# A decoder layer's residual stream kept in DRAM through its mixer, with the attention's output added there by transfers

## The chip, the cores and the metric

The kernel runs on one core of a Trainium2 chip. The metric is the device time of one execution in microseconds (us); lower is better. A core has a matrix engine (TensorE, PE in the profile; its weight loads are PEld), a vector engine (VectorE, DVE), an activation engine (ScalarE, ACT), a general engine (GpSimd, POOL) and a queue engine (SyncE, SP). Transfers are issued from SP, ACT or POOL and run on 16 DMA engines.

## The reference

One decoder layer on x of 512 tokens by 1024 channels, in float32. Each `rms_norm` is a root-mean-square norm.

```python
x = x + 0.5 * swiglu(rms_norm(x, norm_ffn1_w), ffn1_w_in, ffn1_w_out)
x = x + hybrid_mixer(rms_norm(x, norm_mix_w), ...)
x = x + memory_cross_attention(rms_norm(x, norm_cross_w), rms_norm(mem, norm_mem_w), ...)
x = x + 0.5 * swiglu(rms_norm(x, norm_ffn2_w), ffn2_w_in, ffn2_w_out)
return rms_norm(x, norm_final_w)
```

The mixer has two parts that share an input and an output projection: a state-space scan with 16 heads in 4 groups (with a depthwise convolution and a gate z), and differential attention with 8 heads:

```python
z, xbc, dt_raw, q, k, v = split_sizes(h @ w_in, IN_SIZES)
...
return jnp.concatenate([y_ssd, y_attn], axis=-1) @ w_out
```

## The kernel before

**Tiles.** The residual stream x lies transposed: eight tiles of 128 channels by 512 tokens, `x[0]` to `x[7]`, two by two in four pair tiles `x2` of 128x1024. The stream is "column o" for `x[o]`. Each product is done in three float32r matmuls, since each operand is split into a high and a low part (`wh`, `wl` for weights: `wh` by ScalarE at L154, `wl` by VectorE at L155). A weight tile arrives by a load on SP's queue into one of six buffers `wr` (L173).

**Order.** `Order` interleaves two kinds of generators: `od.add` queues dense work (projections), `od.spawn` starts side chains that take a step when the dense work has come far enough by an estimate of matmul time. SP and POOL execute in exactly the order in which the code names their instructions. For PE, DVE and ACT a scheduler picks the order from its own estimates. Each engine then runs its list strictly in order and waits at semaphores.

**Buffers.** Products go into PSUM banks: `acc` has four, `aux` four. Most working tiles are 128x512 and come from the pool `sp` by `s2`, 53 slots (`NSLOT`) under one tag, handed on when the last reader is done. A pool's tag has buffers of its own that no other tag uses.

**The work around the change**, in the order of the dense queue: the first FFN ends with column updates and `fin1`, which spawns `normed` (the mixer's norm, making the eight tiles `h`) and `block_sums_in_dram`, a background chain: SP copies blocks of the second FFN's weights into DRAM tiles `isum` and `wsum` (L1224) and POOL adds other blocks to them there by accumulating transfers (L1228). Then come the cross memory's keys, `queries_keys`, `values`, the groups of the scan (`group_dense`, `group`) and, between them, `out_attn(hg, o0, o1)`: the attention half `hg` (four heads) times its rows of the output projection, columns o0 to o1-1, each a product `pm` of 12 matmuls (weights `woa`), which VectorE adds to `x[o]` (L840). It is called for (0, 0 to 8) after group 0, (1, 0 to 5) after group 1, and (1, 5 to 8) after group 3. Next `memory_values` makes the cross memory's values (products `pcv`, weights `wcv`), and `out_proj` with `upd_c` projects the scan's outputs `ys` (weights `wos`), adds them to `x[o]` (L1092) and makes the cross attention's input from it. Between the norm of the mixer and `upd_c` nothing reads x but these adds.

In a scan group, the chain on POOL is `ysq` (the sum of two squares, L992) and `ncol` (a power, L379), on which later matmuls wait; `pst`, `pf`, `py` are small matmuls, `st` the scan's state, and `conv` (L857) begins the convolution of a product `pxbc`. In the attention heads POOL computes `rr`.

Of the kernel before, what the change touches and what calls it, by code (L numbers as in the profile page):

```python
# [11 lines left out]
F32 = mybir.dt.float32  # L12
R32 = mybir.dt.float32r
AF = mybir.ActivationFunctionType
ALU = mybir.AluOpType
AX = mybir.AxisListType

P = 128
T = 512
D = 1024  # L20
KT = D // P
# [78 lines left out]
def body(tc, a, dbg=None):  # L100
    nc = tc.nc
    ctx = ExitStack()
    ctx.enter_context(tc.manual_schedule(engines={mybir.EngineType.SP, mybir.EngineType.Pool}))
    cp = ctx.enter_context(tc.tile_pool(name="cp", bufs=1))
    wp = ctx.enter_context(tc.tile_pool(name="wp", bufs=3))
    sp = ctx.enter_context(tc.tile_pool(name="sp", bufs=NSLOT))
# [3 lines left out]
    dram = ctx.enter_context(tc.tile_pool(name="dram", bufs=1, space=bass.MemoryType.DRAM))  # L110
# [3 lines left out]
    def nm(s):  # L114
        uid[0] += 1
        return f"{s}_{uid[0]}"

    def s2(s, dt=F32, shape=(P, T)):
        if math.prod(shape[1:]) <= T // 2:
            return sp.tile(list(shape), dt, tag="s1", name=nm(s), bufs=NHALF)  # L120
        return sp.tile(list(shape), dt, tag="s2", name=nm(s))
# [7 lines left out]
    def acc(s, shape=(P, T)):  # L129
        return acc_p.tile(list(shape), F32, tag="acc", name=nm(s))  # L130
# [4 lines left out]
    def dump(name, t):  # L135
        if dbg and name in dbg:
            nc.sync.dma_start(dbg[name], t.bitcast(F32) if t.dtype == R32 else t)

    last, start, last_sum, recent, newest, newest_lo, newest_mm = [], [], [], [], [], [], []
    V, S, G = nc.vector, nc.scalar, nc.gpsimd  # L140
    od = Order()
# [9 lines left out]
    def split_into(hi, lo, src, scale=None):  # L151
        if scale is None:
            return (
                S.activation(hi, src, AF.Copy),  # L154
                V.tensor_tensor(lo, src, hi.bitcast(F32), ALU.subtract),  # L155
            )
        return (
            S.activation(hi, src, AF.Copy, scale=scale),
            V.scalar_tensor_tensor(lo, src, scale, hi.bitcast(F32), ALU.mult, ALU.subtract),
        )  # L160

    def split(s, src, scale=None, half=False, n=T):
        if half:
            both = s2(s, R32, (P, 2, T // 2))
            hi, lo = both[:, 0], both[:, 1]
        else:
            hi, lo = s2(s + "h", R32, (P, n)), s2(s + "l", R32, (P, n))
        last[:] = [i.ins for i in split_into(hi, lo, src, scale)]
        return hi, lo

    def load_w(src, n=D):
        raw = wp.tile([P, n], F32, tag="wr", name=nm("wr"), bufs=6)
        nc.sync.dma_start(raw, src)  # L173
        hi = wp.tile([P, n], R32, tag="wh", name=nm("wh"))
        lo = wp.tile([P, n], R32, tag="wl", name=nm("wl"))
        with ExitStack() as after:
            for i in start:
                after.enter_context(tc.issue_after(i))
            recent[:] = [i.ins for i in split_into(hi, lo, raw)]
        return hi, lo  # L180
# [152 lines left out]
    def mm3(ps, w, x, first, last, wc=slice(None), xc=slice(None)):  # L333
        (wh, wl), (xh, xl) = w, x
        mm(ps, wh[:, wc], xh[:, xc], first, False)
        mm(ps, wh[:, wc], xl[:, xc], False, False)
        mm(ps, wl[:, wc], xh[:, xc], False, last)

    def proj(ps, w, xs, ks=None):
        n = len(xs)  # L340
        for k in ks or range(n):
            mm3(ps, w, xs[k], k == 0, k == n - 1, wc=slice(k * P, (k + 1) * P))
            yield
# [2 lines left out]
    par = cp.tile([P, NPAR], F32, name="par")  # L346
    nc.sync.dma_start(par, a["par"])
    x, wa = [], []
    x2 = [cp.tile([P, 2, T], F32, name=f"x{k}") for k in range(KT // 2)]
    for k in range(KT):  # L350
        xk = x2[k // 2][:, k % 2]
        (S if k == 0 else nc.sync).dma_start(xk, a["xT"][k])
# [62 lines left out]
    def make_h(k, c):  # L415
        return split("hm", x[k], par[:, c + k : c + k + 1])

    def normed(st, c, dst):

        yield from st.finish()  # L420
        hf = {}
        for k in range(KT + 1):
            if k < KT:
                hf[k] = s2("hf")
                V.scalar_tensor_tensor(hf[k], x[k], par[:, c + k : c + k + 1], st.row, ALU.mult, ALU.mult)
            if k > 0:
                dst.append(split("hn", hf.pop(k - 1)))
                yield 1.6
# [140 lines left out]
    with tc.issue_after(start[0]):  # L569
        for k in range(KT):  # L570
            st1.add(x[k])
    st_mix, h = Stat(), []

    def beside(ti):
        if ti == 0:
            od.spawn(memory_norm())
        elif ti == 2:
            od.spawn(memory_prep(hm, 2.5), 10.0)

    def fin1(o):  # L580
        st_mix.add(x[o])
        if o == KT - 3:
            od.spawn(normed(st_mix, C_MIX, h), 3.0)
            od.spawn(block_sums_in_dram(), 60.0)

    od.spawn(st1.finish(), 18.0)
    od.add(ffn1(h1, wa_s, fin1, beside))


# [244 lines left out]
    def out_attn(hg, o0, o1):  # L834
        yield lambda: all(y is not None for y in ya[4 * hg : 4 * hg + 4])
        heads = ya[4 * hg : 4 * hg + 4]
        for o in range(o0, o1):
            po = acc("pm")
            yield from proj(po, load_w(a["woa"][hg, o], 4 * P), heads)
            V.tensor_tensor(x[o], x[o], po, ALU.add)  # L840
        if o1 == KT:
            ya[4 * hg : 4 * hg + 4] = [None] * 4

# [208 lines left out]
    def memory_values():  # L1052
        pv = [[acc("pcv") for _ in range(2)] for _ in range(2)]
        def part(k, w, tb, n):
            mm3(pv[tb][n], hm2[k], w, k == 0, k == KT - 1, wc=slice(tb * P, (tb + 1) * P), xc=slice(n * T, (n + 1) * T))

        banks = [(tb, n) for tb in range(2) for n in range(2)]
        for k in range(KT - 2):
            w = load_w(a["wcv"][k])
            for tb, n in banks:  # L1060
                part(k, w, tb, n)
                yield
        ws = [load_w(a["wcv"][k]) for k in range(KT - 2, KT)]
        for tb, n in banks:
            for j in range(2):
                part(KT - 2 + j, ws[j], tb, n)
                yield
            if n == 0:
                cv.append([])
            cv[tb].append(split("cv", pv[tb][n], st_mem.col[:, tb : tb + 1]))  # L1070
        hm2.clear()
# [17 lines left out]
    st_c, h_c = Stat(), []  # L1089

    def upd_c(o, po):
        V.tensor_tensor(x[o], x[o], po, ALU.add)  # L1092
        h_c.append(make_h(o, C_CROSS))
        st_c.add(x[o])
        dump(f"x2_{o}", x[o])
        if o == KT - 1:
            h.clear()
            od.spawn(st_c.finish(), 3.0)
# [6 lines left out]
    for hd in range(1, 4):  # L1105
        od.add(queries_keys(hd))
    od.add(group_dense(0))
    od.add(out_attn(0, 0, 8))
    od.add(queries_keys(4))
    od.add(values(1))  # L1110
    for hd in range(5, 8):
        od.add(queries_keys(hd))
    od.add(group_dense(1))
    od.add(out_attn(1, 0, SPLIT))
    od.add(group_dense(2))
    od.add(group_dense(3))
    od.add(out_attn(1, SPLIT, 8))
    od.add(memory_values())
    od.add(out_proj(ys, a["wos"], lambda: all(y is not None for y in ys), upd_c))


# [89 lines left out]
    def block_sums_in_dram():  # L1211
        jobs = []
        for c, (f0, nf) in enumerate(THIRDS):
            gs = range(f0 // 2, (f0 + nf) // 2)
            jobs += [(isum[g][0], a["f2q"][g][0], a["f2q"][g][1]) for g in gs]
            jobs += [(isum[g][1], a["f2q"][g][2], isum[g][0]) for g in gs]
            blocks, sums = a[f"f2b{c}"], wsum[c]
            for t, (to, more) in enumerate(((blocks[B12], blocks[B11]), (blocks[B12], blocks[B22]), (blocks[B22], sums[0]), (blocks[B21], sums[2]))):
                for k in range(0, nf // 2 * T, D):
                    ks = slice(k, min(k + D, nf // 2 * T))  # L1220
                    jobs.append((sums[t][:, ks], to[:, ks], more[:, ks]))
        for n in range(len(jobs) + LEAD):
            if n < len(jobs):
                nc.sync.dma_start(jobs[n][0], jobs[n][1])  # L1224
                yield 4.5
            if n >= LEAD:
                to, _, more = jobs[n - LEAD]
                G.dma_start(to, more, accum_op=ALU.add, max_dma_last_dim=4 * D)  # L1228
                yield 8.0
# [262 lines left out]
```

## Time and profile before

| | |
|---|---|
| Three runs | 1307.47, 1308.36, 1309.42 us |
| Profiled execution | 1306.71 us, span 1304.7 us |
| Instructions in the span | 20807 |
| Mean granted TensorE clock | 0.998 |
| Moved by DMA | 229.03 MB, mean 176 GB/s |
| HBM | read 225.53 MB, written 50.91 MB |

The span goes from the first to the last instruction. In the lines of the profile, "busy" is time in which an engine has work, and a name such as `x<-x,pm` says what an instruction writes and reads, buffer numbers left out. Waits are given as total, times and longest. A "q" behind an engine's name marks an instruction of its sequencer, such as the issue of a transfer.

### The profile page before, as it was taken

The numbers are of one execution on the slowest core, as the hardware profiler recorded it, in microseconds if no ns is written. First come the engines' busy times: TensorE is split into PE (matmuls) and PEld (weight loads), VectorE is DVE, ScalarE is ACT, GpSimd is POOL, SyncE is SP. The second block draws the span as 40 slices with busy tenths as digits, with TensorE's granted clock in tenths as the row PEclk, the third lists the DMA queues.
The fourth block names the chain that finished last, engine by engine and source line by source line (L and its number), as shares of the span: only waits on it lengthen the run. The fifth ranks groups of instructions, "written<-read, shape, count | busy, mean of one in ns | idle before, by whom it ended". The sixth has DMA issues, their size and how long they took to land.

```text
span 1304.7 us, 20807 instructions
## 1 busy us (share of the span) xinstructions
PE 1292.8 (99%) x8108; PEld 1150.9 (88%) x8108; DVE 969.6 (74%) x1520; ACT 695.3 (53%) x1183; POOL 108.9 (8%) x127
## 2 busy tenths in 40 slices
PE   9999999999999999999999999999999999999997
PEld 7889999999987788887888888888899999989995
DVE  6886888788884787548877796656677878877886
ACT  6444654556553666336564564434465645555564
POOL 1010010000010011200101012020011000000001
PEclk9999999999999999999999999999999999999999
DMA  8156667767664434953468379594239875655662
GB/s 310 49 192 170 191 166 196 186 182 195 186 232 151 129 90 118 265 182 93 117 182 246 105 174 260 188 225 143 69 106 253 223 229 168 191 201 172 191 204 91
DMA packets 69729, 229.03 MB, mean 176 GB/s; under 512 B 8616, under 2 KB 12176, under 8 KB 69280
## 3 DMA queue, kind: packets, MB, share of 16 engines
q1 hardware_dynamic: 52832, 176.26, 38.7%
q0 software_dynamic: 13056, 44.65, 18.9%
q10 hardware_dynamic: 3744, 6.82, 1.7%
q8 instruction: 63, 1.03, 0.3%
q14 instruction: 34, 0.28, 0.1%
HBM read 225.53 MB, written 50.91 MB: 212 GB/s over the span
## 4 chain that ended last, share of the span: by engine, by line
PE 90%; issue 6%; DVE 2%; ACT 1%; POOL 1%; POOLq 0%; ACTq 0%; DVEq 0%
PE qb L252 15%; PE pm L145 10%; PE qa L252 10%; PE qe L252 10%; PE pxbc L145 5%; PE pcq L145 3%; PE pz L145 3%; PE po L145 3%; PE ob L1258 3%; PE pv L145 3%; PE oa L1258 2%; PE pq L145 2%; PE oe L1258 2%; PE pk L145 2%; PE pa L145 2%
## 5 line engine op out<-in xcount | busy, mean ns | idle before, releaser
L154 ACT ACTIVATE wh<-wr 128x1024 fp32r<-128x1024 f32 (+2 forms) x323 | 329.3, 1022 | 355.6 <-issue 95.7
L155 DVE TENSOR_TENSOR wl<-wr,wh 128x1024 fp32r<-128x1024 f32 (+2 forms) x323 | 379.7, 1178 | 144.6 <-ACT wh L154 138.6
L145 PE MATMUL pxbc<-hnh,wh 128*128 128x512 f32 x128 | 52.9, 413 | 0.0
L252 PE MATMUL qb<-s24h,wl 128*128 128x256 f32 x184 | 52.2, 284 | 0.2 <-DVE wl L155 0.2
L252 PE MATMUL qb<-s24h,wh 128*128 128x256 f32 x184 | 52.4, 285 | 0.0
L252 PE MATMUL qb<-s24l,wh 128*128 128x256 f32 x184 | 52.2, 284 | 0.0
L252 PE MATMUL qb<-s31h,wh 128*128 128x256 f32 x184 | 52.2, 283 | 0.0
L252 PE MATMUL qe<-s31h,wh 128*128 128x256 f32 x184 | 52.1, 283 | 0.0
L252 PE MATMUL qb<-s31l,wh 128*128 128x256 f32 x184 | 52.1, 283 | 0.0
L252 PE MATMUL qe<-s24l,wh 128*128 128x256 f32 x184 | 52.1, 283 | 0.0
L252 PE MATMUL qe<-s24h,wh 128*128 128x256 f32 x184 | 52.1, 283 | 0.0
L252 PE MATMUL qb<-s31h,wl 128*128 128x256 f32 x184 | 52.1, 283 | 0.0
L252 PE MATMUL qe<-s31l,wh 128*128 128x256 f32 x184 | 52.1, 283 | 0.0
L252 PE MATMUL qe<-s24h,wl 128*128 128x256 f32 x184 | 52.1, 283 | 0.0
L252 PE MATMUL qe<-s31h,wl 128*128 128x256 f32 x184 | 52.1, 283 | 0.0
L145 PE MATMUL pxbc<-hnh,wl 128*128 128x512 f32 x128 | 50.2, 392 | 0.0
L145 PE MATMUL pxbc<-hnl,wh 128*128 128x512 f32 x128 | 49.9, 390 | 0.0
L754 ACT ACTIVATE ec<-ec,mn 128x512 f32<-128x512 f32 (+3 forms) x64 | 35.5, 556 | 25.7 <-DVE mn L753 25.6
L252 PE MATMUL qa<-h11h,wh 128*128 128x256 f32 x152 | 43.1, 283 | 0.0
L252 PE MATMUL qa<-h11h,wl 128*128 128x256 f32 x152 | 43.0, 283 | 0.0
L252 PE MATMUL qa<-h11l,wh 128*128 128x256 f32 x152 | 43.0, 283 | 0.0
L860 DVE SCALAR_TENSOR_TENSOR conv<-pxbc,par,conv 128x511 f32<-128x511 f32 (+2 forms) x48 | 35.8, 746 | 6.5 <-ACT conv L857 5.7
(490 smaller groups left out, 4171.0 us busy)
## 6 DMA issues: line engine op xcount, KB each, us to landing
wr<-in_f2q SPq DMA_DIRECT2D x44, 512.0 KB, 4.2
wr<-in_f1q SPq DMA_DIRECT2D x40, 512.0 KB, 4.5
isum<-in_f2q SPq DMA_DIRECT2D x22, 512.0 KB, 5.3
wr<-isum SPq DMA_DIRECT2D x22, 512.0 KB, 4.2
wr<-in_f1o SPq DMA_DIRECT2D x20, 512.0 KB, 3.9
wsum<-in_f2b SPq DMA_DIRECT2D x20, 512.0 KB, 6.6
wr<-wsum SPq DMA_DIRECT2D x20, 512.0 KB, 4.3
wr<-in_f1q POOLq DMA_DIRECT2D x16, 512.0 KB, 5.7
```

Of the source, the lines that this page charges most:

```text
L145: newest_mm[:] = [nc.tensor.matmul(out, w, x, start=start, stop=stop).ins]
L154: S.activation(hi, src, AF.Copy),
L155: V.tensor_tensor(lo, src, hi.bitcast(F32), ALU.subtract),
L252: newest_mm[:] = [nc.tensor.matmul(out, a_[:, wc], b_, start=first and f == 0 and kp == 0 and j == 0, stop=kp == n - 1 and j == 2, skip_gr ...
L754: S.activation(ec[:, :n], ec[:, :n], AF.Exp, bias=mn, scale=-1.0, accum_out=sm[c][:, i : i + 1])
L860: V.scalar_tensor_tensor(y[:, d:], ps[:, : T - d], par[:, cw + j : cw + j + 1], y[:, d:], ALU.mult, ALU.add)
L1258: newest_mm[:] = [nc.tensor.matmul(ps, a_[:, ts], b_[:, ws], start=first and k == 0 and j == 0, stop=k == n - 1 and j == 2, skip_group_che ...
```

## The change

The four pair tiles move from their fixed place into a tag `x2` of the pool `sp` with four buffers. A chain `x_away`, spawned by `fin1`, waits until the eight tiles `h` of the mixer's norm are made and stores the four pairs into a DRAM tile `x_d`. In `out_attn` ScalarE copies each product `pm` into a working tile `xo`, and POOL issues an accumulating transfer that adds it to the column in `x_d`. `x_back` loads one pair; it is called in `memory_values` after the last weight load, and in `upd_c` before columns 0, 2 and 4, each time for the next pair. `upd_c` adds to the loaded columns as before.

```diff
-    x2 = [cp.tile([P, 2, T], F32, name=f"x{k}") for k in range(KT // 2)]
+    def pair_tile():
+        return sp.tile([P, 2, T], F32, tag="x2", name=nm("x2"), bufs=KT // 2)
+
+    x2 = [pair_tile() for _ in range(KT // 2)]
...
+    x_d = dram.tile([KT // 2, P, 2, T], F32, name="x_d")
+
+    def x_away():
+        while len(h) < KT:
+            yield 1.0
+        for n in range(KT // 2):
+            nc.sync.dma_start(x_d[n], x2[n])
+            yield 2.5
+        x2.clear()
+        x.clear()
+
+    def x_back():
+        n = len(x2)
+        x2.append(pair_tile())
+        nc.sync.dma_start(x2[n], x_d[n])
+        x.extend(x2[n][:, j] for j in range(2))
...
             od.spawn(normed(st_mix, C_MIX, h), 3.0)
+            od.spawn(x_away(), 40.0)
             od.spawn(block_sums_in_dram(), 60.0)
...
             yield from proj(po, load_w(a["woa"][hg, o], 4 * P), heads)
-            V.tensor_tensor(x[o], x[o], po, ALU.add)
+            part = s2("xo")
+            S.activation(part, po, AF.Copy)
+            G.dma_start(x_d[o // 2, :, o % 2], part, accum_op=ALU.add)
...
         ws = [load_w(a["wcv"][k]) for k in range(KT - 2, KT)]
+        x_back()
...
     def upd_c(o, po):
+        if o % 2 == 0 and len(x2) < KT // 2:
+            x_back()
         V.tensor_tensor(x[o], x[o], po, ALU.add)
```

Instructions move at few places; the number of matmuls stays, and PE's list differs only beside group 3. There, on PE, the products `pm` of columns 6 and 7 (here numbered 8314 and 8340) stood before like this, with the scan's `pst` and two `pcv` between:

```order
L145 MATMUL pm_8314<-yah_7325,wl_8318 128x512
L145 MATMUL pm_8340<-yah_6732,wh_8343 128x512
L145 MATMUL pm_8340<-yal_6733,wh_8343 128x512
L145 MATMUL pcv_8393<-wh_8399,hm_8067 128x512
L145 MATMUL pcv_8394<-wh_8399,hm_8067 128x512
L145 MATMUL pst_8301<-xde_8237,btk_8277 128x256
L145 MATMUL pst_8308<-xde_8237,btk_8277 128x256
L145 MATMUL pst_8324<-xde_8252,btk_8277 128x256
L145 MATMUL pm_8340<-yah_6732,wl_8344 128x512
L145 MATMUL pm_8340<-yah_6922,wh_8343 128x512
```

Now, with column 7's product numbered 8375:

```order
L145 MATMUL pm_8375<-yah_6753,wh_8378 128x512
L145 MATMUL pm_8375<-yal_6754,wh_8378 128x512
L145 MATMUL pm_8375<-yah_6753,wl_8379 128x512
L145 MATMUL pm_8375<-yah_6943,wh_8378 128x512
L145 MATMUL pm_8375<-yal_6944,wh_8378 128x512
L145 MATMUL pm_8375<-yah_6943,wl_8379 128x512
L145 MATMUL pm_8375<-yah_7161,wh_8378 128x512
L145 MATMUL pm_8375<-yal_7162,wh_8378 128x512
L145 MATMUL pm_8375<-yah_7161,wl_8379 128x512
L145 MATMUL pst_8332<-xde_8268,btk_8308 128x256
L145 MATMUL pst_8339<-xde_8268,btk_8308 128x256
L145 MATMUL pst_8357<-xde_8283,btk_8308 128x256
```

The three `pst` moved behind seven more matmuls of column 7, and the two `pcv` moved behind the whole product. On ACT, at the same place, before:

```order
L848 ACTIVATE th_1641_8282<-pz_8179 128x512
L909 ACTIVATE e_1660_8356<-th_8036 64x512
L946 ACTIVATE st_8303<-pst_8301 128x256
L911 ACTIVATE th_8036<-th_8036,cum 128x128 x4
L909 ACTIVATE e_1660_8356<-th_8036 64x512
L912 ACTIVATE th_8036<-th_8036 128x512
L911 ACTIVATE th_8036<-th_8036,cum 128x128 x4
L912 ACTIVATE th_8036<-th_8036 128x512
```

And now, with the copies of columns 5, 6 and 7 as `xo`:

```order
L870 ACTIVATE th_1658_8313<-pz_8210 128x512
L861 ACTIVATE xo_8344<-pm_8316 128x512
L968 ACTIVATE st_8334<-pst_8332 128x256
L861 ACTIVATE xo_8372<-pm_8347 128x512
L931 ACTIVATE e_1679_8391<-th_8067 64x512 x2
L933 ACTIVATE th_8067<-th_8067,cum 128x128 x5
L934 ACTIVATE th_8067<-th_8067 128x512
L933 ACTIVATE th_8067<-th_8067,cum 128x128 x3
L861 ACTIVATE xo_8427<-pm_8375 128x512
L934 ACTIVATE th_8067<-th_8067 128x512
```

One copy stands ahead of the state's copy `st`, and the third ahead of the last exponential. On SP, from the last `wcv` loads to the first `wos` loads, before:

```order
L173 DMA wr_8537<-in_wcv 128x1024
L1224 DMA isum_257<-in_f2q 16x8192
L173 DMA wr_8595<-in_wos 128x1024
L173 DMA wr_8601<-in_wos 128x1024
L1224 DMA isum_259<-in_f2q 16x8192
L173 DMA wr_8688<-in_wos 128x1024
L173 DMA wr_8728<-in_wos 128x1024
L173 DMA wr_8767<-in_wos 128x1024
L1224 DMA isum_261<-in_f2q 16x8192
```

Now:

```order
L173 DMA wr_8574<-in_wcv 128x1024
L590 DMA x_1717_8580<-x_d 128x1024
L1249 DMA isum_258<-in_f2q 16x8192
L173 DMA wr_8634<-in_wos 128x1024
L173 DMA wr_8640<-in_wos 128x1024
L590 DMA x_1742_8704<-x_d 128x1024
L1249 DMA isum_260<-in_f2q 16x8192
L173 DMA wr_8729<-in_wos 128x1024
L590 DMA x_1753_8760<-x_d 128x1024
L173 DMA wr_8771<-in_wos 128x1024
L173 DMA wr_8810<-in_wos 128x1024
L1249 DMA isum_262<-in_f2q 16x8192
```

Three of the four loads of `x_d` stand among the first five `wos` loads; the fourth follows this piece. On POOL, the accumulating transfers of the first half's columns 5 to 7 stand between `ysq` and `ncol` of group 0, the other thirteen ahead of a `ysq`. Since the copies take slots of the pool `sp`, later instructions that get such a slot wait for the transfer that read it: among them, on ACT, the first `conv` of group 2 (for column 2 of the second half) and the second (for column 4).

## The prediction

> **What bounds the kernel now.** I read the page first: the busy shares, the granted clock and the heads of the chain of waits.
>
> ```profile
> PE 1292.8 (99%) x8108; PEld 1150.9 (88%) x8108; DVE 969.6 (74%) x1520; ACT 695.3 (53%) x1183; POOL 108.9 (8%) x127
> PEclk9999999999999999999999999999999999999999
> PE 90%; issue 6%; DVE 2%; ACT 1%; POOL 1%; POOLq 0%; ACTq 0%; DVEq 0%
> ```
>
> TensorE is busy for 1292.8 of 1304.7 us at full clock in every slice, and the chain that ended last is 90% matmuls. Next I read the waits of PE, which are all that the profile lists for it:
>
> ```profile
> PE init L366 <- DVE ones_r L364: 1.5, 1, 1.5
> PE ptk L149 <- ACT of L810: 0.6, 1, 0.6
> PE qb L252 <- DVE wl L155: 0.2, 1, 0.2
> ```
>
> None of them is at a line that the change touches. Third came the sums by stretch, for the four places where the change acts: the first half of the attention's projection (505 to 545), five columns of the second half (665 to 690), its last three columns beside group 3 (755 to 780), and the memory values with the start of the last projection (780 to 810). The columns are length, busy time of PE, weight load, DVE, ACT and POOL with counts, clock, DMA share and GB/s.
>
> ```profile
> 505.00:545.00 40.00, 40.00 (x219) 33.44 (x218) 25.88 (x41) 19.03 (x40) 3.62 (x4) 1.00 0.73 227
> 665.00:690.00 25.00, 25.00 (x140) 20.73 (x139) 19.85 (x31) 14.42 (x31) 0.72 (x1) 1.00 0.73 238
> 755.00:780.00 25.00, 24.90 (x133) 20.21 (x134) 23.30 (x42) 19.51 (x43) 3.11 (x3) 1.00 0.73 176
> 780.00:810.00 30.00, 30.00 (x155) 25.05 (x154) 19.87 (x24) 13.31 (x16) 6.14 (x6) 1.00 0.84 252
> ```
>
> PE is full in all four; only 755 to 780 lacks 0.10 us. There DVE is close to full too (23.30 of 25), so that is the one place where work taken from DVE could be felt. The view of line 840, the add that goes, says how much:
>
> ```profile
> L840 DVE TENSOR_TENSOR x<-x,pm x16: 677/688/689, 514.1 to 779.2; 128x512 f32<-128x512 f32 x16
>   PE pm L145: 5.8, 11
>   PEld pcv L145: 0.5, 1
> ```
>
> DVE waits for PE before eleven of the sixteen adds, and PE waits once for an add: 0.5 us, by its weight load for `pcv`. The chain shows that spot:
>
> ```profile
> 769.92 0.70 DVE x L840
> 770.67 0.50 PE pcv L145
> 771.19 1.56 PE pst L145 x6
> ```
>
> A `pcv` matmul needed the PSUM bank that a late add still held.
>
> **The change part by part.** The number of matmuls stays; the path is PE, so each part is priced by what it makes PE wait.
>
> *The adds go.* 16 x 0.688 = 11.0 us of DVE, of which 0.5 us lies on the path: at 770 PE no longer starts `pcv` there, but goes on with `pm`, and `pcv` comes when its banks are long free. Gain 0.5 us. The other fifteen are covered by four rotating PSUM banks: gain 0.
>
> *The copies come.* The nearest row is a ScalarE copy of the same shape out of PSUM:
>
> ```profile
> L810 ACT ACTIVATE of<-po 128x512 f32<-128x512 f32 x8 | 4.7, 582 | 3.5 <-PE po L145 3.5
> ```
>
> 16 x 0.58 = 9.3 us of ACT. Each frees its bank after 0.58 instead of 0.69 us. In 505 to 545, eight copies make 19.03 + 4.7 = 23.7 of 40 us; in 665 to 690 five make 17.3 of 25; in 755 to 780 three make 21.2 of 25. ACT runs in order, and in the last stretch the first copy stands ahead of `st<-pst`, for which `pf` on PE waits. Bounds: 0 if ACT's free time takes them, 3 x 0.58 = 1.7 us if all three push the work behind them onto PE. I take 0, since `pst` itself comes later by seven `pm` matmuls in the new order, so the copy has run before `st` can start.
>
> *POOL issues sixteen accumulating transfers.* The rows of such issues, and of the arithmetic that stands behind them on POOL:
>
> ```profile
> 756.76 1.72 POOL L1228 DMA_DIRECT2D wsum<-in_f2b  x2
> 534.46 1.54 POOL L992 TENSOR_TENSOR ysq<-ysq,ysq 128x512 f32<-128x512 f32 x1 [33.09 <-ACT ysq L990]
> 543.67 1.03 POOL L379 TENSOR_TENSOR ncol<-nv,mhalf 128x4 f32<-128x4 f32 x1 [6.92 <-DVE nv L377]
> 788.95 1.82 POOL L992 TENSOR_TENSOR ysq<-ysq,ysq 128x512 f32<-128x512 f32 x1 [30.47 <-ACT ysq L990]
> ```
>
> 16 x 0.86 = 13.8 us of POOL. An issue waits for its copy, and POOL holds everything behind it. What PE later needs is `ysq` and `ncol`. Before `ysq` at 534.46 POOL idles 33.09 us, before the one at 788.95 30.47 us, and before `ncol` at 543.67 6.92 us. Ahead of that `ncol` now stand the last three issues of the first half; their last copy can start when the add at 537.9 did, so POOL is free at 537.9 + 0.6 + 0.9 = 539.4. Cost 0. The background sums of weights wait longer, and they are read only in the second FFN.
>
> ```profile
> 537.88 0.69 DVE L840 TENSOR_TENSOR x<-x,pm 128x512 f32<-128x512 f32 x1 [0.58 <-PE pm L145]
> ```
>
> *A buffer is held until the transfer has landed.* Each copy takes one of the 53 slots (128x512, f32) of the working pool. In the new order later ScalarE instructions, two `conv` of group 2 among them, wait for the transfers of columns 2 and 4 of the second half. The landing time of an accumulation into DRAM is bounded by two rows of the same size, and the moments by the adds and the `conv` of before:
>
> ```profile
> wsum<-in_f2b POOLq DMA_DIRECT2D x2, 256.0 KB, 7.2
> wsum<-wsum POOLq DMA_DIRECT2D x2, 256.0 KB, 9.1
> ...
> 678.53 0.69 DVE L840 TENSOR_TENSOR x<-x,pm 128x512 f32<-128x512 f32 x1 [0.23 <-PE pm L145]
> 683.99 0.69 DVE L840 TENSOR_TENSOR x<-x,pm 128x512 f32<-128x512 f32 x1 [0.63 <-PE pm L145]
> ...
> 692.15 0.76 ACT L857 ACTIVATE conv<-pxbc,par 128x512 f32<-128x512 f32 x1
> 697.54 0.76 ACT L857 ACTIVATE conv<-pxbc,par 128x512 f32<-128x512 f32 x1
> ```
>
> With the slower row: 678.5 + 0.6 + 0.9 + 9.1 = 689.1, which is 3.0 us before 692.15; and 684.0 + 10.6 = 694.6, 2.9 us before 697.54. Cost 0; each us beyond 12 us of landing time would delay a bank's release, and three other banks cover that first. The Trainium skill, in "DMA: Bandwidth & Descriptors", section "Anatomy of one DMA", gives a POOL-issued transfer 2.0 us plus its bytes by 436 GB/s, an estimate of 2.6 us here. The trace has 7.2 to 9.1 us, so the measurement decides; by the page the margin would be some 9 us, and the sum the same.
>
> *The stream goes out and comes back.* Four stores and four loads of 512 KB on SP's queue, each issue under 0.5 us of SP like its neighbours. The stores stand among the loads of `wv`; nothing waits for them but the first accumulation, over 100 us later. The loads come back ahead of the `wos` weights:
>
> ```profile
> 781.47 2.21 SPq L173 DMA_DIRECT2D wr<-in_wos  x2
> 783.73 0.49 SPq L1224 DMA_DIRECT2D isum<-in_f2q  x1
> 784.96 7.75 SPq L173 DMA_DIRECT2D wr<-in_wos  x3
> 792.76 0.49 SPq L1224 DMA_DIRECT2D isum<-in_f2q  x1
> ...
> wr<-in_wos SPq DMA_DIRECT2D x8, 512.0 KB, 5.6
> ...
> L145 PE MATMUL pm<-ysh,wh x64: 389/389/478, 801.6 to 845.4; 128*128 128x512 f32 x64
> L1092 DVE TENSOR_TENSOR x<-x,pm x8: 680/689/689, 812.3 to 846.3; 128x512 f32<-128x512 f32 x8
> ```
>
> The last pair is the one that could hold SP: its load waits for column 7, whose add ended at 779.2 + 0.7 in the old kernel, so its accumulation lands at 779.2 + 0.6 + 0.9 + 9.1 = 789.8. SP reaches this load after the 792.76 row, so it does not stop. The first weights need 781.47 + 5.6 = 787.1, PE uses them from 801.6: 14.5 us of cover. The pairs themselves are read by the adds from 812.3 on. Cost 0; without that cover the late thing would be the `wos` cast, then PE.
>
> **Sum.** -0.5 + 0 + 0 + 0 + 0 = -0.5 us. The profiled execution took 1306.7 us (span 1304.7 and 2.0 around it), so it would take 1306.2. It ran 1.65 us under the median of the runs, so on the median's footing it is 1308.36 - 0.5 = 1307.9 us. A difference under 0.2%, 2.6 us, can't be told from none here.
>
> **The rivals.** First, *DVE's relief pays more*. For it: DVE is 74% busy and 23.30 of 25 us in one stretch. Against it: PE's idle time in the four stretches is 0.10 us in all. If each of sixteen banks, freed 0.11 us earlier, were felt, it would give 1.8 us more: 1306.1 us, still inside the band. To leave it, the whole 11.0 us would have to count: 1297.4 us.
>
> Second, *ScalarE becomes what PE waits for*. For it: 755 to 780 leaves ACT little room, and slots are now handed on by transfers. Against it: the margins above. Three copies on the path give 1307.9 + 1.7 = 1309.6 us; all sixteen, or `conv` held at both tight places, up to 1307.9 + 9.3 = 1317.2 us. It decides once a landing takes over 12 us.
>
> Third, and on the slower side, *the transfers crowd out the weights*. The DMA queues of the page:
>
> ```profile
> q1 hardware_dynamic: 52832, 176.26, 38.7%
> q0 software_dynamic: 13056, 44.65, 18.9%
> ```
>
> SP's queue spends 0.387 x 1304.7 / 176.26 = 2.9 us of all 16 engines per MB, POOL's 5.5. Between 755 and 810 three accumulations (0.79 MB, 4.3 us) and four loads (2.1 MB, 6.0 us) are added: 10.3 us. Free there is 25 x 0.27 + 30 x 0.16 = 11.6 us. So the engines would be full for some 50 us. If the added 10.3 us all delay one weight, 14.5 us of cover still hold; beyond that PE stops for the rest, and with two such loads in a row 1307.9 + 2 x 10.3 - 14.5 = 1314.0 us. The same page of the Trainium skill, section "Issuing engines are not separate DMA queues", speaks for this rival: transfers of SP, ACT and POOL run on the same 16 engines and interleave, so a second queue brings no bandwidth. That the trace agrees is seen in stretches of full share, but no wait of PE for a load is in its list.
>
> Last, *nothing usable is freed*: the four pair buffers keep a tag of their own and the working pool keeps its 53 slots, so no buffer gains from the absent stream. That ends within the band too, and is part of the forecast.
>
> **How the numbers follow.** Forecast within the band 0.82 (with the small forms of the first two rivals); DVE's relief beyond the band 0.06; ScalarE or slots beyond it 0.05; transfers beyond it 0.07. So faster 0.06, same 0.82, slower 0.12. The low end is the first rival's 1306.1; the high end is the highest run shown, 1309.42, with three copies on the path less the gain, +1.7 - 0.5: 1310.6. The 0.18 outside are the large forms.
>
> **What would show it.** After the change line 840's adds are gone from DVE (969.6 down by about 11), ACT is up by about 9 and POOL has sixteen more issues near 0.86 us; PE stays at 99%, and the chain near 770 has no DVE piece. Wrong would be: PE waits at `pf`, `pxbc` or `pm` by ScalarE, `wh<-wr` waiting for a `wos` or `wcq` load before 860, or accumulations landing after more than 12 us.

## The result and the profile after

The changed kernel took 1303.31 us (1303.24 to 1303.99, five runs) against 1308.36 (1307.06 to 1309.42, five runs) of the kernel before on the same chip: a ratio of 0.9964, 95% interval 0.9951 to 0.9977. It is faster by 5.0 us or 0.36%; the forecast was 1307.9 us, no change, and 1303.31 lies below its range. Its profiled execution took 1303.58 us, with a span of 1301.0, 3.7 us shorter than before.

The page of the changed kernel, heads and queues:

```profile
span 1301.0 us, 20886 instructions
PE 1290.8 (99%) x8108; PEld 1150.2 (88%) x8108; DVE 959.6 (74%) x1504; ACT 703.3 (54%) x1199; POOL 122.5 (9%) x143
q1 hardware_dynamic: 53984, 180.45, 39.6%
q0 software_dynamic: 15360, 48.84, 20.5%
PE 90%; issue 6%; DVE 2%; ACT 1%; POOL 1%; POOLq 0%; ACTq 0%; DVEq 0%
```

The counts are as forecast: DVE has 16 instructions and 10.0 us less, ACT 16 and 8.0 us more, POOL 16 and 13.6 us more. PE has the same 8108 matmuls, but is busy 2.0 us less. These totals don't show where PE gained; that must be found by place. The four stretches of the prediction, now of the changed kernel (length, busy time of PE, weight load, DVE, ACT, POOL; clock, DMA share, GB/s):

```profile
505.00:545.00 40.00, 40.00 (x218) 33.46 (x217) 20.88 (x33) 23.13 (x47) 11.71 (x14) 1.00 0.85 229
665.00:690.00 25.00, 25.00 (x139) 20.63 (x138) 16.01 (x25) 16.39 (x34) 6.34 (x7) 1.00 0.78 190
755.00:780.00 25.00, 25.00 (x139) 21.05 (x138) 23.00 (x40) 21.14 (x46) 5.43 (x6) 1.00 0.63 181
780.00:810.00 30.00, 30.00 (x155) 25.07 (x154) 17.94 (x22) 12.25 (x15) 6.13 (x6) 1.00 1.03 327
```

In 755 to 780 PE makes 139 matmuls instead of 133; elsewhere the counts agree within one. By the moments at which the same matmuls start, three places make 3.1 of the span's 3.7 us; most of the rest (0.5 us) is the program's start, which varies from execution to execution.

**First place: beside group 3.** The chain of waits, two pieces of the kernel before and then five of the changed kernel (start, length, what):

```profile
764.41 5.49 PE pm L145 x24
785.63 11.80 PE pcv L145 x51
```

```profile
763.75 7.51 PE pm L145 x33
771.26 1.29 PE pst L145 x6
772.55 0.22 PE pf L145 x2
772.77 1.02 PE py L145 x16
783.68 11.80 PE pcv L145 x51
```

From column 5's product to the long run of `pcv` it was 785.63 - 764.41 = 21.22 us, and is 783.68 - 763.75 = 19.93: 1.29 us gained. What PE's matmuls lost there does not stand in PE's own waits, of which the profile lists none in this stretch; most of it stands in those of its weight load. Before (763 to 787), then after:

```profile
PEld pcv L145 <- DVE x L840: 0.5, 1, 0.5
PEld pst L145 <- ACT btk L937: 0.3, 1, 0.3
PEld pf L145 <- DVE st L954: 0.2, 1, 0.2
PEld pm L145 <- issue: 0.2, 1, 0.2
PEld pcv L145 <- issue: 0.2, 1, 0.2
```

```profile
PEld pm L145 <- issue: 0.2, 1, 0.2
PEld pcv L145 <- issue: 0.2, 1, 0.2
```

Three waits are gone: for the late add (0.50 us), for `btk`, an operand of `pst` that ScalarE copies out of PSUM (0.33), and for a state `st` from VectorE (0.17). They are 1.0 us in all, beside 1.29 us gained. `btk` is ready 6.7 us after the start of column 5's product in both kernels; with more `pm` matmuls ahead of `pst` it is there in time now, and the six `pst` take 1.29 us and not 1.56. The rest of the gain, 0.3 us or a little more, has no wait in the profile. `py`, which ran in pieces of 14 and 2 matmuls, now runs in one of 16; whether that is the reason, no run shows.

**Second place: the end.** The closing instructions of POOL's and SP's sequencers (shortest, median and longest in ns; first and last start in us), before and after:

```profile
L1488 POOLq DRAIN  x3: 51/98/6384, 1297.6 to 1304.5; - x3
L1488 SPq DRAIN  x3: 7/7/7, 1302.5 to 1304.2; - x3
```

```profile
L1513 POOLq DRAIN  x3: 51/98/3769, 1295.3 to 1300.8; - x3
L1513 SPq DRAIN  x3: 7/7/7, 1300.2 to 1300.5; - x3
```

Before, SP was done at 1302.5, the outputs being landed, but POOL's drain of 6.38 us ran to 1303.9 and the program ended at 1304.7: 2.2 us after SP. Now POOL's drain takes 3.77 us and is over before SP's; the program ends 1301.0 - 1300.2 = 0.8 us after SP. That is 1.4 us gained.

**Third place: the second FFN.** The unchanged kernel, in another profiled execution (the first run below), has this in its chain:

```profile
1020.55 1.51 PE qb L252 x13
1022.06 0.03 issue
1022.08 0.68 DVE s24l L155
1022.76 0.74 DVE wl L155
1023.50 0.32 issue
1023.82 0.68 DVE gl L155
1024.50 0.61 DVE c L325
...
1025.24 3.11 PE qb L252 x24
```

The same stretch of the changed kernel has matmuls alone:

```profile
1018.33 2.88 PE qb L252 x24
1021.21 1.44 PE qe L252 x12
1022.64 2.88 PE qb L252 x24
```

A weight comes late there. ScalarE's waits in 1010 to 1030 of that execution have this row, and the changed kernel has no such row there:

```profile
ACT wh L154 <- DMA wr<-in_f2q: 2.3, 1, 2.3
```

Some 40 us earlier, transfers of the same stage land later than in the changed kernel. That they are what delays the weight is argued from the order of time; no run shows it. The issue of one POOL transfer near 974 us, before and then after (KB, us to landing):

```profile
wsum<-in_f2b POOLq DMA_DIRECT2D x1, 512.0 KB, 7.8
```

```profile
wsum<-in_f2b POOLq DMA_DIRECT2D x1, 512.0 KB, 5.6
```

From the last product of the cross attention's output projection to the last matmul it took 331.09 us in the profile before, 331.53 in the repeated one and 330.72 after.

### The profile page after: what moved, and what is told of

Its sections match the earlier page's. It is cut to its first block, busy times and chain, and to the rows that moved or that the text cites. A ratio compares the mean times of both kernels' runs of the same rounds, so it can differ in the third digit from the quotient of the medians.

```text
span 1301.0 us, 20886 instructions
## 1 busy us (share of the span) xinstructions
PE 1290.8 (99%) x8108; PEld 1150.2 (88%) x8108; DVE 959.6 (74%) x1504; ACT 703.3 (54%) x1199; POOL 122.5 (9%) x143
## 3 DMA queue, kind: packets, MB, share of 16 engines
q8 instruction: 63, 1.03, 0.3%
## 4 chain that ended last, share of the span: by engine, by line
PE 90%; issue 6%; DVE 2%; ACT 1%; POOL 1%; POOLq 0%; ACTq 0%; DVEq 0%
PE qb L252 15%; PE pm L145 10%; PE qa L252 10%; PE qe L252 10%; PE pxbc L145 5%; PE pcq L145 3%; PE pz L145 3%; PE po L145 3%; PE ob L1283 3%; PE pv L145 3%; PE oa L1283 2%; PE pq L145 2%; PE oe L1283 2%; PE pk L145 2%; PE pa L145 2%
## 5 line engine op out<-in xcount | busy, mean ns | idle before, releaser
L154 ACT ACTIVATE wh<-wr 128x1024 fp32r<-128x1024 f32 (+2 forms) x323 | 329.0, 1022 | 348.5 <-issue 98.4
```

## The experiments

Every kernel was timed beside the kernel before on the same chip, and each difference is to those runs. "Stage" is the time from column 5's product to the long run of `pcv`, as above (from the chain), "drain" the longest of POOL's closing instructions, "landing" the time that the `wsum` transfer near 974 us took to land; "FFN2" is the time from the last product of the cross attention's output projection to the last matmul. Some expectations count otherwise: their drain begins at the end of POOL's last operation and is 1.02 us shorter (5.36 for 6.38 us), and their time from column 5 runs to the last value product (37.2 us before).

| Kernel | Median, us | Against before, us | 95% of the ratio | Stage | Drain | Landing | FFN2 |
|---|---|---|---|---|---|---|---|
| before, once more | 1307.85 | -0.1 | 0.9994 to 1.0012 | 21.19 | 6.38 | 7.4 | 331.53 |
| copy, then add | 1306.03 | -1.9 | 0.9978 to 0.9996 | 20.06 | 6.38 | 7.4 | 331.86 |
| three copies | 1306.55 | -1.0 | 0.9982 to 1.0000 | 20.06 | 6.38 | 7.8 | 331.43 |
| accumulation in SBUF | 1305.60 | -2.4 | 0.9972 to 0.9990 | 19.94 | 3.77 | 7.3 | 333.70 |
| sixteen POOL issues | 1306.41 | -1.6 | 0.9981 to 1.0000 | 21.23 | 3.52 | 7.4 | 332.00 |
| eight POOL issues | 1308.16 | -0.2 | 0.9988 to 1.0006 | 21.22 | 6.87 | 7.5 | 332.38 |
| changed, once more | 1303.43 | -3.9 | 0.9963 to 0.9984 | 19.94 | 3.77 | 6.1 | 330.66 |
| round trip alone | 1306.57 | -0.8 | 0.9986 to 1.0004 | 21.19 | 6.38 | 5.8 | 330.69 |
| x in the other pool | 1306.91 | -0.5 | 0.9992 to 1.0009 | 21.23 | 6.38 | 7.5 | 331.43 |
| stores alone | 1306.48 | -0.9 | 0.9986 to 1.0003 | 21.23 | 6.38 | 6.0 | 330.67 |
| stores, tile behind | 1306.36 | -1.2 | 0.9979 to 0.9997 | 21.20 | 6.38 | 6.0 | 330.74 |
| four tiny stores | 1307.68 | -0.7 | 0.9985 to 1.0003 | 21.22 | 6.38 | 7.4 | 332.30 |
| tile, one tiny store | 1306.19 | -2.2 | 0.9975 to 0.9993 | 21.22 | 6.38 | 6.1 | 330.99 |
| SBUF, and stores | 1303.14 | -4.4 | 0.9951 to 0.9976 | 19.94 | 3.77 | 5.9 | 330.67 |
| changed, more issues | 1303.39 | -4.2 | 0.9949 to 0.9976 | 19.94 | 2.63 | 6.0 | 331.04 |
| three parts, no relief | 1303.14 | -5.2 | 0.9950 to 0.9975 | 20.05 | 3.53 | 5.4 | 330.70 |

**The kernel before once more**, unaltered.

> The kernel before, unchanged, once more. Theory A (the gain belongs to the program: TensorE's order beside group 3, 1.2 us, and the end of the execution, 1.4 us, where POOL's last drain took 6.4 us before and 3.8 us after): 1308.4 us +-1, and the profile shows POOL's drain at the end near 6.4 us again and the stall at 770 again. Rival B (the end and the start differ from execution to execution by chance): POOL's drain or the first matmuls move by 0.5 us or more between this profile and the first one, and the time may be 1306 to 1309 us.

1307.85 us, the same as its neighbours. The stage and the drain repeat, the landing is 7.4 after 7.8 us, and the second FFN's wait is there, near 1022 us. Of the 0.6 us between the two spans, the second FFN makes 0.44.

### TensorE's order

**Copy, then add.** x stays in SBUF; ScalarE copies each product and VectorE adds the copy. VectorE loses no add.

```diff
-            V.tensor_tensor(x[o], x[o], po, ALU.add)
+            part = s2("xo")
+            S.activation(part, po, AF.Copy)
+            V.tensor_tensor(x[o], x[o], part, ALU.add)
```

> The stream stays in SBUF; ScalarE copies each attention product and VectorE adds the copy to the stream, so the PSUM bank is freed by ScalarE and VectorE keeps its sixteen adds; POOL has no new work. TensorE's list beside group 3 is near that after the change. Theory A: about half of the gain, some 1.2 us under the control by TensorE's order, with POOL's drain at the end as in the control. Rival C (the relief of VectorE itself pays): no gain, within 0.5 us of the control, since the sixteen adds are still there.

1306.03 us, and the stage falls from 21.2 to 20.06 us with DVE busy for 969.4 us. The bank is freed by another engine and the scheduler puts PE's instructions in another order. In this order the waits for the add, `btk` and `st` are gone from the weight load, with VectorE as busy as before. The engine that frees the bank and the order change together in all these runs, so none tells the two apart.

**Three copies.** The same for columns 5 to 7 of the second half alone.

```diff
-            V.tensor_tensor(x[o], x[o], po, ALU.add)
+            if hg == 1 and o >= SPLIT:
+                part = s2("xo")
+                S.activation(part, po, AF.Copy)
+                V.tensor_tensor(x[o], x[o], part, ALU.add)
+            else:
+                V.tensor_tensor(x[o], x[o], po, ALU.add)
```

`SPLIT` is 5.

> The kernel before, but in the last three of the sixteen columns (5 to 7 of the second half) ScalarE copies the product and VectorE adds the copy to x; thirteen adds, and everything else, as before. TensorE's list is word for word that of the run with sixteen copies. Theory A (TensorE's order beside the last group of heads is what pays, and three columns set it): from column 5 to the last value product 36.0 to 36.1 us instead of 37.2, total 1306.0 to 1306.5 us, as with sixteen copies. Rival C (VectorE's relief in all sixteen columns): no stage shorter, 1307.2 to 1307.6 us.

PE's list is that of the sixteen copies. Its chain:

```profile
764.20 7.52 PE pm L145 x33
784.26 11.80 PE pcv L145 x51
```

784.26 - 764.20 = 20.06 us, exactly as with sixteen copies: thirteen of the sixteen have no part in it. The total is 1.0 us less, and the interval reaches 1: an effect of 1.2 us is at the edge of what these times resolve, so the stage decides.

### POOL's drain

**Accumulation in SBUF.** ScalarE's copies and POOL's accumulating transfers as in the changed kernel, but onto x in SBUF; no round trip.

```diff
-            V.tensor_tensor(x[o], x[o], po, ALU.add)
+            part = s2("xo")
+            S.activation(part, po, AF.Copy)
+            G.dma_start(x[o], part, accum_op=ALU.add)
```

> The stream stays in SBUF; ScalarE copies each product and POOL's accumulating transfers add it to the stream there. TensorE's list is word for word that of the changed kernel; no stream goes to DRAM or comes back. Theory A: the whole gain, 1303 to 1304.5 us, because TensorE's order and POOL's list are those of the changed kernel. Rival D (the stream's absence from SBUF, or its eight transfers, matter): 1306 us or more.

1305.60 us: stage and drain are the changed kernel's, DVE is busy for 959.4 us as there, and yet only 2.4 us are won, which lies between the ranges of theory A and of rival D. In this profile FFN2 took 333.70 us, 3.0 us longer than in the changed kernel, so the rest of the gain was to be looked for there.

**Sixteen POOL issues.** The kernel before, with a transfer of 128x4 to an unread DRAM tile behind each add.

```diff
             V.tensor_tensor(x[o], x[o], po, ALU.add)
+            G.dma_start(idle_d[hg, o], mhalf)
```

> The kernel before with sixteen small transfers (128x4, from a constant into DRAM) issued by POOL, one behind each add; TensorE's list is word for word that of before. Theory A's second half (the number of POOL's transfers sets how long POOL drains at the end): POOL's last drain falls from 6.4 to about 3.8 us and the time by 1.4 us, to 1307 us. If it doesn't depend on that: drain and time as in the control, 1308.4 us.

The drain falls to 3.52 us:

```profile
L1490 POOLq DRAIN  x3: 51/98/3522, 1298.1 to 1303.6; - x3
```

The median is 1.6 us lower. As expected, sixteen transfers that do nothing shorten the end as the sixteen accumulations do; stage and landing stay as before.

**Eight POOL issues.** Those of the first half alone.

```diff
+            if hg == 0:
+                G.dma_start(idle_d[hg, o], mhalf)
```

> The kernel before plus eight tiny POOL transfers, in the first half's eight columns only; sixteen of them cut POOL's last drain from 5.36 to 2.50 us, and sixteen besides the sixteen accumulations to 1.61. Theory D1 (the more POOL has issued, the shorter): 3 to 4.5 us, 1306.4 to 1307.2 us. Theory D2 (position in a ring, or a threshold between 8 and 16): 5.36 us, 1307.4 us, or 2.5 us, 1306.2.

```profile
L1491 POOLq DRAIN  x3: 51/97/6872, 1298.7 to 1306.1; - x3
```

Not shorter but half a microsecond longer. "The more, the shorter" falls in this form, and the values that theory D2 named aren't met either.

**The changed kernel with more issues.** Sixteen tiny transfers beside the sixteen accumulations.

```diff
             G.dma_start(x_d[o // 2, :, o % 2], part, accum_op=ALU.add)
+            G.dma_start(idle_d[hg, o], mhalf)
```

> The changed kernel plus sixteen tiny POOL transfers (128x4), one behind each accumulation: POOL has 32 more transfers than before instead of 16. POOL's drain at the end took 5.36 us in kernels with the transfers of before and 2.50 to 2.75 us with 16 more. Theory D1 (the more, the shorter): under 1.5 us, 1302.6 to 1303.4 us in all. Theory D2 (it hangs on the count modulo a ring, or on one position in it): another value, perhaps 5 us again and 1304.5 to 1305 us. Theory D3 (what counts is that POOL was kept busy with any transfers there): 2.5 to 2.8 us, 1303.2 to 1303.7 us.

```profile
L1515 POOLq DRAIN  x3: 51/93/2626, 1295.9 to 1301.4; - x3
```

2.63 us, but 1303.39 us in all, no gain over 1303.31 and 1303.43: at 3.77 us the drain already ended before the last output had landed. POOL issued 90 transfers before, and 98, 106 and 122 here: 6.38, 6.87, 3.5 to 3.8 and 2.63 us. The drain was 6.38 us in all ten profiles with 90 transfers, whatever else had changed, so it goes with the number of transfers, but not in proportion; by which rule stays open.

### The second FFN

**The changed kernel once more**, unaltered.

> The changed kernel once more, unaltered, on the chip and beside the run of the kernel before. Of its 5 us two parts are shown in other runs: 1.27 us by TensorE's order in the last group of heads, 1.42 us by POOL's last drain. The other 2.3 us lie in the second feed-forward, where every other profile has a wait for `wr<-in_f2q` near 1018 to 1024 us (0.5 to 1.6 us) and this one had none. Theory A (the change brings this too): 1303 to 1304 us again, spread under 1 us, no such wait. Rival B (luck of five runs): median 1304.5 to 1306, spread of 3 us as in the kernel before, the wait back in the profile.

1303.43 us, landing 6.1 us, and no wait near 1020 us: the change does bring this part, it was not luck of the first runs. The runs spread over 2.0 us, more than theory A said.

**The round trip alone.** The stream goes out, comes back ahead of the first output projection, and VectorE makes its adds in SBUF. Against the changed kernel:

```diff
         heads = ya[4 * hg : 4 * hg + 4]
+        while len(x2) < KT // 2:
+            x_back()
...
-            part = s2("xo")
-            S.activation(part, po, AF.Copy)
-            G.dma_start(x_d[o // 2, :, o % 2], part, accum_op=ALU.add)
+            V.tensor_tensor(x[o], x[o], po, ALU.add)
...
         ws = [load_w(a["wcv"][k]) for k in range(KT - 2, KT)]
-        x_back()
...
-        if o % 2 == 0 and len(x2) < KT // 2:
-            x_back()
```

> The round trip of the stream alone: four stores after the norm, four loads back ahead of the first output projection, VectorE's sixteen adds kept; every engine's order is that of the kernel before, SP has eight transfers more. No part of the 2.7 us (TensorE's order, POOL's drain) is in it: 5.36 us of drain, 37.2 us from column 5 to the last value product. Theory A1 (the DRAM tile and SP's transfers are what frees the second feed-forward): 1305.0 to 1306.2 us, with a spread under 1.5 us and no wait near 1020. Rival A2 (something else does): 1307 to 1308.5 us, with the wait.

**x in the other pool.** The kernel before with the pair tiles of x from the tag `x2` of the pool `sp`.

```diff
-    x2 = [cp.tile([P, 2, T], F32, name=f"x{k}") for k in range(KT // 2)]
+    x2 = [sp.tile([P, 2, T], F32, tag="x2", name=nm("x2"), bufs=KT // 2) for _ in range(KT // 2)]
```

> The kernel before with x's four pair tiles taken from the pool that the changed kernel takes them from; nothing else moves, every engine's list is the same, only addresses in SBUF differ. Theory A3 (where x and the tiles of that pool lie in SBUF sets how fast the weights of the second feed-forward land): 1305 to 1306.2 us with a spread under 1.5 us. Otherwise 1307 to 1308.5 us as before.

**The stores alone.** The four stores of `x_away` into `x_d`, x kept in SBUF; against the kernel before.

```diff
+    x_d = dram.tile([KT // 2, P, 2, T], F32, name="x_d")
+
+    def x_away():
+        while len(h) < KT:
+            yield 1.0
+        for n in range(KT // 2):
+            nc.sync.dma_start(x_d[n], x2[n])
+            yield 2.5
...
+            od.spawn(x_away(), 40.0)
             od.spawn(block_sums_in_dram(), 60.0)
```

> The kernel before plus the stream's DRAM tile of 2 MB and the four stores into it, which nobody reads; x stays in SBUF. Every engine's order is that of before, SP has four transfers more and what is allocated in DRAM behind that tile (the sums of the second feed-forward's weights) lies elsewhere. Theory A1 by place in DRAM: 1305 to 1306.2 us and a small spread, as in the round trip. Theory A1 by the number of SP's transfers (eight are needed, or loads): 1306 to 1307.5. Otherwise 1307 to 1308.5 us.

The place of x in SBUF does nothing: landing 7.5 us, time as before. The trip and the stores alone both have landings of 5.8 and 6.0 us and the shortest FFN2. In time each is 0.8 to 0.9 us lower, with no change still inside the interval, and the trip's 1306.57 us lies between the ranges of its two theories; so the times don't decide here, and the reading rests on the profile. Beside four profiles that have no such tile, the difference shows at 975 to 982 us: six transfers in a row take 1.6 to 3.3 us less in the mean.

**The stores, with the tile behind.** The tile `x_d` declared after `isum` and `wsum`; against the stores alone.

```diff
-    x_d = dram.tile([KT // 2, P, 2, T], F32, name="x_d")
...
     wsum = [[dram.tile([P, nf // 2 * T], F32, name=f"wsum{c}{t}") for t in range(4)] for c, (_, nf) in enumerate(THIRDS)]
+    x_d = dram.tile([KT // 2, P, 2, T], F32, name="x_d")
```

> The four stores as in the run of the stores alone, but their DRAM tile is allocated behind the sums of the second feed-forward's weights instead of ahead of them, so that those lie where they do in the kernel before. With the tile ahead (four profiles) the transfer `wsum<-in_f2b` issued near 974 us landed in 5.6 to 6.1 us and the stage from the last product of the scan's projection on took 330.7 us; without it (six profiles) 7.3 to 7.8 us and 331.1 to 333.7. Theory A1a (the place of the sums in DRAM): 7.3 to 7.8 us, 331 us or more, the wait back, 1307.4 us median as before. Theory A1b (the four stores themselves, or the position of SP's queue): 5.6 to 6.1 us, 330.7 us, 1306.5 us.

The expectation says "the scan's projection" for FFN2's first edge; it is the cross attention's. Landing 6.0 us, FFN2 330.74, 1306.36 us: theory A1a falls, the order in which the tiles are declared does not matter.

**Four tiny stores.** As many transfers, 128x4 each, into a tile of 8 KB. This and the next edit are against the stores alone.

```diff
-    x_d = dram.tile([KT // 2, P, 2, T], F32, name="x_d")
+    x_d = dram.tile([KT // 2, P, 4], F32, name="x_d")
...
-            nc.sync.dma_start(x_d[n], x2[n])
+            nc.sync.dma_start(x_d[n], mhalf)
```

> Four stores on SP's queue at the same place as in the run of the stores alone, but of 128x4 each into a tile of 8 KB: the number of SP's transfers without the bytes and without the 2 MB in DRAM. Theory S1 (the number of SP's transfers, so the position of its queue): the transfer `wsum<-in_f2b` issued near 975 us lands in 5.6 to 6.1 us, the last stage 330.7 us, 1306.3 to 1306.6 us. Theory S2 (2 MB more in DRAM, wherever the tile stands, move what lies there): 7.3 to 7.8 us, 331 us or more, 1307.4 us.

**The tile with one tiny store.** 2 MB, of which 2 KB are written.

```diff
-        for n in range(KT // 2):
-            nc.sync.dma_start(x_d[n], x2[n])
-            yield 2.5
+        nc.sync.dma_start(x_d[0, :, 0, :4], mhalf)
+        yield 2.5
```

> The 2 MB tile in DRAM with a single store of 128x4 into it: the allocation, with SP's transfers one more than before. Theory S1 (the number of SP's transfers): 7.3 to 7.8 us for the transfer near 975 us, or between if one counts a quarter; 1307.2 to 1307.5 us. Theory S2 (the allocation): 5.6 to 6.1 us, 330.7 us, 1306.3 to 1306.6 us.

The same row as above, of the four tiny stores and then of the big tile with one:

```profile
wsum<-in_f2b POOLq DMA_DIRECT2D x1, 512.0 KB, 7.4
```

```profile
wsum<-in_f2b POOLq DMA_DIRECT2D x1, 512.0 KB, 6.1
```

The allocation shortens the landing, not the transfers: 1306.19 us, 2.2 us less, an interval clear of 1. By their times alone the four tiny stores (-0.7 us) and the stores alone (-0.9) could not be told apart. Over all profiles, landing is 7.3 to 7.8 us in nine without the 2 MB tile and 5.4 to 6.1 in nine with it, and FFN2 takes 331.09 to 333.70 against 330.66 to 331.04 us. ScalarE's wait for a weight `wr<-in_f2q` between 1000 and 1035 us is in eight of the nine without the tile and in none of the nine with it. Which address the tile moves, and why those six transfers mind, no run shows.

### The parts together

**Accumulation in SBUF, and the stores.** The edits of those two runs together: neither loads back nor accumulation in DRAM.

> x stays in SBUF, ScalarE copies each product, POOL's sixteen accumulating transfers add it there (this alone gave -2.4 us), and the four stores into a DRAM tile that nobody reads are put in as well (alone -0.9 us). TensorE's order is that of the changed kernel. Theory A (three separate parts: TensorE's order 1.2 to 1.3 us, POOL's drain 1.4 us, the second feed-forward's weights 0.4 to 1.5 us; none needs the stream to be away): 1303.3 to 1304.2 us, no wait near 1020, the transfer `wsum<-in_f2b` issued near 973 us lands in 5.6 to 6.1 us. Rival (accumulating in DRAM instead of SBUF, or the loads back, matter by themselves): 1304.8 to 1306 us.

1303.14 us: the changed kernel's time with the stream in SBUF throughout.

**The three parts without the relief.** Three copies, sixteen tiny POOL transfers, four stores that nobody reads; VectorE makes all sixteen adds. Beside the lines of the stores alone:

```diff
-            V.tensor_tensor(x[o], x[o], po, ALU.add)
+            if hg == 1 and o >= 5:
+                part = s2("xo")
+                S.activation(part, po, AF.Copy)
+                V.tensor_tensor(x[o], x[o], part, ALU.add)
+            else:
+                V.tensor_tensor(x[o], x[o], po, ALU.add)
+            G.dma_start(idle_d[hg, o], mhalf)
```

> The three parts without the thing itself: x stays in SBUF and VectorE makes all sixteen adds; ScalarE copies the product of the last three columns, POOL issues sixteen tiny transfers that nobody reads, SP stores the stream four times where nobody reads it. Theory A (TensorE's order 1.2, POOL's drain 1.4, the second feed-forward 0.4 to 1.5 us): 1303.2 to 1304.2 us, as the changed kernel, with VectorE as busy as before (968 us or more). Rival (some of the changed kernel's gain does come of the adds' removal): 1304.5 us or more.

```profile
PE 1290.9 (99%) x8108; PEld 1150.6 (88%) x8108; DVE 969.4 (75%) x1520; ACT 697.2 (54%) x1186; POOL 117.8 (9%) x143
```

1303.14 us (1302.79 to 1306.46) with VectorE as busy as before. The whole gain is there and not one add is gone: VectorE's relief, the first rival, is worth nothing that can be measured. None of the runs is faster than the changed kernel by more than their spread, so no better version follows.

## Why the prediction was wrong

- *The adds go, gain 0.5 us.* The place and the sign were right, the size was not: the stage became 1.29 us shorter. The step priced the one wait for an add and took PE's own three rows for all that PE waits for. The weight load's rows of the same profile also have the waits for `btk` (0.33 us) and `st` (0.17) at this place, and the new order ends those too; some 0.3 us stay without a wait that explains them. The order came from ScalarE's copies in three columns, not from DVE's 11 us, of which nothing measurable was gained.
- *The sum.* The larger failed step is that it had no term for the end of the program and none for the second FFN. The sixteen POOL issues were weighed for what stands behind them on POOL (0, and that was right: no `ysq` or `ncol` is waited for) but not for POOL's own closing drain, 1.4 us. The rows of the drain were in the trace of before: POOL ended 1.4 us after SP.
- *The stream goes out and comes back, 0.* For SP, the stores and the loads that was right: PE waits for nothing there. But the tile's allocation was not seen as part of the change. With the tile FFN2 takes 330.76 us in the mean of nine profiles, without it 331.97, a gain of 1.2 us; how the tile does it stays open.
- 1.3 + 1.4 + 1.2 = 3.9 us; measured were 5.0, and 3.9 in the repeat, where the spread of the kernel before alone is 3.3 us. The sum of the prediction had the right sign, but for the two larger parts, which it didn't foresee, that is luck.
- *The copies, 0.* Right: sixteen copies of 0.58 us, and no wait of PE by them.

```profile
L861 ACT ACTIVATE xo<-pm x16: 576/580/599, 513.8 to 776.7; 128x512 f32<-128x512 f32 x16
```

- *Slots held until the landing, 0.* Right in effect. The bounds of 7.2 and 9.1 us from the nearest rows held for the median, not for the longest, which is at the 12 us named as the point of decision. The Trainium skill's "Anatomy of one DMA" in "DMA: Bandwidth & Descriptors" gave an estimate of 2.6 us, and the trace has three times that at the median.

```profile
x_d<-xo POOLq DMA_DIRECT2D x16, 256.0 KB, 8.1
...
DMA to landing us min/median/max: 4.0/8.1/12.0
```

- *The third rival's mechanism took place and cost PE nothing that the profile shows.* From 780 to 810 the DMA share rose from 0.84 to 1.03 and the `wos` loads from 5.6 to 10.1 us at the median; PE has no wait for a `wos` weight. The longer landings agree with what the Trainium skill, "DMA: Bandwidth & Descriptors", section "Issuing engines are not separate DMA queues", says: transfers of all issuing engines share the same 16 DMA engines.

```profile
wr<-in_wos SPq DMA_DIRECT2D x8, 512.0 KB, 10.1
```

- *The band.* Same 0.82 and faster 0.06 rested on the four stretches where the change acts. Two of three effects lay outside them.

## What to carry to other kernels

When PE is 99% busy, read the waits of its weight load as well as its own, and ask of each one near a changed order whether it stays. Look at the last few microseconds as at any stage: which engine's closing instruction ends last, and what the change does to it. And where an edit allocates in DRAM or changes the count of an engine's transfers, time that alone, with the data path as before, before the gain is put down to what the edit was for.

## What was not expected of the hardware

- POOL's closing drain takes 2.6 to 6.9 us and goes with the number of transfers that POOL issued in the program: 90, 98, 106 and 122 gave 6.38, 6.87, 3.5 to 3.8 and 2.63 us. The Trainium skill, "VectorE: DVE Perf Modes", section "The DRAIN you can't avoid", tells of drains of about 12 ns on all five engines, from the runtime's preamble and postamble. POOL's drain, at the line that closes the kernel's own program, is hundreds of times that, so that figure is no price for it.
- A 2 MB tile in DRAM, even one that nobody reads, made six transfers of 512 KB, 600 us after the last store into it, land in 4.4 to 7.3 us rather than 7.2 to 9.1 (nine profiles each).
- A stretch in which PE is listed with no wait can still lose time to its weight load: here 1.0 us of its waits stood between 764 and 786 us, and the stage became 1.29 us shorter when they went.
